# New operation costs and delays in the planner of an attention stage's instruction order

## The chip, the cores and the metric

The kernel runs on one core of a Trainium2 chip. The metric is the device time of one execution in microseconds (us); less is better. A core has engines that each work through their own queue of instructions in order and wait for one another only by semaphores: TensorE (PE, matrix products; PEld is its weight load), VectorE (DVE), ScalarE (ACT) and GpSimd (POOL). SyncE (SP), ACT and POOL issue transfers (DMA). Matrix products write to PSUM, which has eight banks of 512 float32 columns; the other engines read the results from there.

## The reference

One block of a network on 1024 tokens of width 1024: a norm, an input projection, two mixers side by side (a chunkwise mLSTM and a sparse attention), a gated sum of the two through `w_branch`, an output projection, a gated feed-forward layer and a last norm. The edit concerns the attention mixer, which for each block of queries computes

```python
lc = einsum('bgrqd,bgcd->bgrqc', qb, kc_) + bias        # compressed keys, branch 0
o_c = softmax(lc) @ vc_
ls = einsum('bgrqd,bgqnd->bgrqn', qb, k_selected) + bias  # selected blocks, branch 1
o_s = softmax(ls) @ v_selected
lw = einsum('bgrqd,bgkd->bgrqk', qb, k_window) + bias     # window of 512, branch 2
o_w = softmax(lw) @ v_window
out = gate0 * o_c + gate1 * o_s + gate2 * o_w
```

with 8 heads in 2 groups. Sixteen blocks of 64 keys exist and the top 16 are selected, so branch 1 sees all keys up to the query. The mixers' outputs then go through `branch = ys @ w_branch`, are multiplied by `sigmoid(merge)` gates and summed.

## The kernel before

All products are made in split float32 parts: a high part (ACT, line 333 for weights, 1623 for attention) and the remainder, the low part (`wlo` on POOL at line 336, `TL` on DVE at line 1627). A dense product of two split operands is a triplet of matmuls of 512 columns (`mm3`, lines 354 to 356).

**Attention.** The work is cut into 32 units `u` = (pair of heads `p`, block of 128 queries `i`). Each unit has, in order:

- logits, `build_s`: for branches 2 and 0 together ("w") and for branch 1 ("s"), for each head `r` of the pair, matmuls into a PSUM tile `S` (lines 1527 and 1528; two such tiles), then on DVE the bias is added and the row's minimum taken (line 1554, "low"), then on ACT the exponential with its row sum (line 1558);
- a normaliser `rs` for each part (lines 1570 and 1571, DVE) and scalings of the exponentials by it: line 1579 on DVE or, as the list chooses (`alt`), line 1577 on ACT;
- groups of one or two key blocks, `build_t`: transposes on TensorE into a PSUM tile `T` (line 1618; two such tiles), the high part `TH` on ACT, the low part `TL` on DVE, and the products with the values into `obank` (lines 1635 with `TH` and 1638 with `TL`); after a unit's last group ACT copies the result (`os`, line 1644), SP writes one half of it to memory and POOL adds the other half.

**Dense filler.** `c_dense` yields dense triplets one at a time: 12 merge groups of 8 triplets, each evicted by ACT with a bias (line 1456, `mg`), then 16 branch groups of 4 triplets, each evicted by DVE (line 1478, `MX`). All of them accumulate in one PSUM bank, the tile `d` (tag `D`, one buffer), so a group can start only when the one before it has been evicted. The weights of later groups are loaded by SP and split by ACT and POOL on the way (`load`, `split`).

**The order.** The attention's instructions are written in the order that a list planner gives. Every operation (`Op`) has an engine, a duration and what it depends on; the planner keeps one clock for each engine and a delay `LAT` that is added when a result goes to another engine. It repeatedly takes, over the three engines PE, ACT and DVE, the operation that can start first, by priority among those that are ready. On PE, a dense triplet is placed if no attention operation can start within 120 ns of the time at which the triplet could. A scaling goes to ACT only if the planner's DVE clock isn't earlier than ACT's start. When the last logits of a pair of heads are through DVE, `load_pair` issues the next pair's loads, and its first logits are held back for 9000 or 17000 ns of planned time (`pair_at`). When attention's queues are empty, dense triplets are written one after another until at least 13 of the 16 branch groups are done:

```python
while not dn["done"] and (done["n"] < 13 or dn["mid"]):
    ev, evict = next(cd)
```

The branch groups still left (`rest`) are handed to the following stage, which has its own planner and eight banks. The engines don't know of the planned times: they keep the order and the semaphores alone.

Of the kernel before, what the change touches and what calls it, by code (L numbers as in the profile page):

```python
# [15 lines left out]
T = 1024  # L16
# [19 lines left out]
MM = 216.0  # L36
# [136 lines left out]
def body(ctx, tc, a, out):  # L173
# [1249 lines left out]
    with ExitStack() as sc:  # L1423
# [138 lines left out]
        def scale(u, part):  # L1562

            p, i = units[u]
            sl = slice(0, 3, 2) if part == 0 else slice(1, 2)
            gt = GT[:, i, 6 * p:6 * p + 6].rearrange("p (r b) -> p r b", b=3)[:, :, sl]

            def first():
                rs, sm = RS[u][:, :, sl], SUM[u][:, :, sl]
                nc.vector.scalar_tensor_tensor(rs, sm, 1.0e-30, gt, ALU.max, ALU.mult)  # L1570
                nc.vector.reciprocal(rs, rs)

            def one(b, r, eng="DVE"):
                n = (ncmp(i), P * (i + 1), P * nwin(i))[b]
                e = EX[u, "c"][:, r, 0:n] if b == 0 else EX[u, "w" if b == 2 else "s", r][:, 0:n]
                if eng == "ACT":
                    nc.scalar.activation(e, e, AF.Copy, scale=RS[u][:, r, b:b + 1])
                else:
                    nc.vector.tensor_scalar(e, e, RS[u][:, r, b:b + 1], None, ALU.mult)

            todo = [(first, None)]
            for b in ((2, 0) if part == 0 else (1,)):
                for r in range(2):
                    todo.append((lambda eng="DVE", b=b, r=r: one(b, r, eng), (u, b) if r == 1 else None))
            return todo
# [78 lines left out]
                self.eng, self.dur, self.deps, self.emit, self.prio = eng, dur, deps, emit, prio  # L1664
                self.end, self.extra, self.alt = None, extra, alt

        LAT = 180.0
        chain = {"S": [], "T": [], "V": []}
        queues = {"PE": [], "ACT": [], "DVE": []}
        clock = {"PE": 0.0, "ACT": 0.0, "DVE": 0.0}  # L1670

        def push(op):
            queues[op.eng].append(op)
            if op.alt:
                queues[op.alt[0]].append(op)
            return op
# [3 lines left out]
        pv_ops, oc_ops = [], {}  # L1680
# [3 lines left out]
        def build_s(u):  # L1684
            p, i = units[u]
            ops = {}
            for k, r in (("w", 0), ("w", 1), ("s", 0), ("s", 1)):
                b = {"w": 2, "s": 1}[k]
                box = {}

                def emit(u=u, k=k, r=r, box=box):
                    box["low"], box["exp"] = s_job(u, k, r)


                if b == 1:
                    n, parts = P * (i + 1), [min(512, P * (i + 1) - c) for c in range(0, P * (i + 1), 512)]
                else:
                    n, parts = P * nwin(i), [P * (nwin(i) - 1)] * (nwin(i) > 1) + [KB]
                cost = 2 * sum(max(109.0, m / 2.4 + 13.0) for m in parts)
                deps = []  # L1700
                if len(s_free) >= 2:
                    deps.append(s_free[-2])
                if u >= 2:
                    deps.append(("T", u - 2, b))
                if u % 8 == 0 and k == "w" and r == 0:
                    deps.append(("pair", p))
                deps += chain["S"]
                so = push(Op("PE", cost, deps, emit, (u, 1)))
                chain["S"] = [so]
                nr, n = (2, n + ncmp(i)) if b == 2 else (1, n)  # L1710
                tt = push(Op("DVE", nr * 180.0 + 1.044 * n, [so], lambda box=box: box["low"](), (u, 1)))
                s_free.append(tt)
                ex = push(Op("ACT", nr * 290.0 + 0.833 * n, [tt], lambda box=box: box["exp"](), (u, 1)))
                ops[k, r] = ex
                if r == 1:
                    part = 0 if k == "w" else 1
                    de = [ops[k, 0], ex]
                    todo = scale(u, part)
                    rs = push(Op("DVE", 400.0, de, todo[0][0], (u, 2)))
                    bl = [2, 2, 0, 0] if part == 0 else [1, 1]  # L1720
                    scd = {}
                    for bb, (fn, _) in zip(bl, todo[1:]):
                        nn = (ncmp(i), P * (i + 1), P * nwin(i))[bb]
                        scd.setdefault(bb, []).append(push(Op("DVE", 70.0 + 0.522 * nn, [rs], fn, (u, 2),
                                                               alt=("ACT", 230.0 + 0.833 * nn))))
                    for bb, v in scd.items():
                        ops["sc", bb] = v
            return ops

        def build_t(u, ops):  # L1730
            p, i = units[u]
            gr = t_groups(u)
            first = True
            for gi, (part, grp) in enumerate(gr):
                box = {}
                m = len(grp)
                last = gi == len(gr) - 1

                def emit(u=u, gi=gi, grp=grp, last=last, box=box):
                    _, box["hi"], box["lo"], box["pv"] = t_job(u, gi, grp, last)  # L1740

                deps = [o for b, _ in grp for o in ops["sc", b]]
                deps += chain["T"]
                t = push(Op("PE", 214.0 * m, deps, emit, (u, 0), "T"))
                chain["T"] = [t]
                for b, _ in grp:
                    last_t[u, b] = t
                nfr = 256.0 * m
                d2 = [t] + ([pv_ops[-NTH]] if len(pv_ops) >= NTH else [])
                hi = push(Op("ACT", 60.0 + 0.833 * nfr, d2, lambda box=box: box["hi"](), (u, 0)))  # L1750
                lo = push(Op("DVE", 75.0 + 1.044 * nfr, [hi], lambda box=box: box["lo"](), (u, 0)))
                t.extra = ("T", lo)
                dp = [lo]
                if first and u >= 2:
                    dp.append(("OC", u - 2))
                first = False

                def emit_pv(box=box):
                    box["fin"] = box["pv"]()

                dp += chain["V"]
                pv = push(Op("PE", 428.0 * m / 2, dp, emit_pv, (u, 3)))
                chain["V"] = [pv]
                pv_ops.append(pv)
                if last:
                    oc_ops[u] = push(Op("ACT", 270.0, [pv], lambda box=box: box["fin"](), (u, 0)))

        for u in range(NU):
            build_t(u, build_s(u))
# [9 lines left out]
        def ready(op, eng):  # L1779
            t = 0.0  # L1780
            for d in op.deps:
                d = dep_op(d)
                if isinstance(d, tuple):
                    e = pair_at.get(d[1])
                else:
                    e = d.end
                    if e is not None and d.eng != eng:
                        e += LAT
                if e is None:
                    return None  # L1790
                t = max(t, e)
            if op.extra is not None and len(talloc) >= 2:
                e = talloc[-2].end
                if e is None:
                    return None
                t = max(t, e + LAT)
            return t

        dstate = {"gate": 0.0, "op": None}
# [1 line left out]
        dn = {"done": False, "mid": False}  # L1801
        split_end = {}

        def dense_at():
            if dstate["op"] is not None:
                o = dstate["op"]
                return None if o.end is None else max(o.end + LAT, split_end.get(dn["next"][1], 0.0) + LAT)
            return dstate["gate"]

        def place_dense(t):  # L1810
            ev, evict = next(cd)
            dn["mid"] = evict is None
            end = clock["PE"] = t + 3 * MM
            dstate["gate"], dstate["op"] = 0.0, None
            if ev is not None:
                clock["ACT"] = max(clock["ACT"], t) + 950.0
                split_end[ev] = clock["ACT"] + 2600.0
            if evict is not None:
                e = dn["next"][0]
                pe = Op("PE", 3 * MM, [], None, (-1, 0))  # L1820
                pe.end = end
                o = Op(e, 587.0 if e == "ACT" else 680.0, [pe], evict, (-1, 0))
                queues[e].insert(0, o)
                dstate["op"] = o
                dn["next"] = next(cd, None)
                dn["done"] = dn["next"] is None
# [5 lines left out]
        while any(queues.values()):  # L1832
# [19 lines left out]
            cand, e = best  # L1852
# [23 lines left out]
        while not dn["done"] and (done["n"] < 13 or dn["mid"]):  # L1876
            ev, evict = next(cd)
# [830 lines left out]
    bb = {}  # L2708
# [68 lines left out]
```

## Time and profile before

| | |
|---|---|
| median of 3 runs | 1515.35 us (1514.84 to 1516.04) |
| profiled execution, span | 1513.3 us |
| TensorE busy | 1495.8 us (99%) |
| VectorE busy | 1137.3 us (75%) |
| ScalarE busy | 829.1 us (55%) |
| GpSimd busy | 311.3 us (21%) |
| HBM read, written | 185.26 MB, 60.39 MB |

The profile gives the span from the first to the last instruction; the time of the timed runs also holds what lies around the span. Matmuls are pipelined: one of 512 columns is shown with some 390 ns, while the next starts some 227 ns after it, so the busy time of TensorE is no measure of how full it is, but its idle time is idle. Rows of the timeline read: start in us, length in us, engine, line, operation, output <- inputs, sizes, count, and in brackets the engine's idle time before it and what ended it. Rows of the stage windows give, for each engine, the busy time and the number of instructions, then the granted TensorE clock as a share of full speed, the DMA engines' busy share and GB/s. Rows of one line or tile give count, then the shortest, median and longest duration in ns, then the first and the last start in us.

### The profile page before, as it was taken

The numbers are of one execution on the slowest core, as the hardware profiler recorded it, in microseconds if no ns is written. First come the engines' busy times: TensorE is split into PE (matmuls) and PEld (weight loads), VectorE is DVE, ScalarE is ACT, GpSimd is POOL, SyncE is SP. The second block draws the span as 40 slices with busy tenths as digits, with TensorE's granted clock in tenths as the row PEclk, the third lists the DMA queues.
The fourth block names the chain that finished last, engine by engine and source line by source line (L and its number), as shares of the span: only waits on it lengthen the run. The fifth ranks groups of instructions, "written<-read, shape, count | busy, mean of one in ns | idle before, by whom it ended". The sixth has DMA issues, their size and how long they took to land.

```text
span 1513.3 us, 22320 instructions
## 1 busy us (share of the span) xinstructions
PE 1495.8 (99%) x7566; PEld 1262.8 (83%) x7566; DVE 1137.3 (75%) x2411; ACT 829.1 (55%) x1753; POOL 311.3 (21%) x389
## 2 busy tenths in 40 slices
PE   8999999999999999999999999999999999999997
PEld 6888888888889888898888788888888888888886
DVE  8979888867678896989787997555555555785795
ACT  6325666657569796878654674333333333454453
POOL 3000000000312243232101422322222221413310
PEclk9999999999999999999999999999999999999999
DMA  8324664496943378442477966877787776999731
GB/s 278 112 78 143 204 211 147 139 262 188 227 148 73 93 103 235 152 103 50 130 222 181 213 122 134 151 138 138 176 157 138 138 139 139 271 303 177 155 96 56
DMA packets 236133, 239.25 MB, mean 158 GB/s; under 512 B 13458, under 2 KB 179744, under 8 KB 236019
## 3 DMA queue, kind: packets, MB, share of 16 engines
q1 hardware_dynamic: 157296, 169.96, 35.4%
q0 software_dynamic: 78432, 67.48, 29.7%
q8 instruction: 59, 0.97, 0.3%
q14 instruction: 56, 0.45, 0.1%
q10 hardware_dynamic: 290, 0.40, 0.1%
HBM read 185.26 MB, written 60.39 MB: 162 GB/s over the span
## 4 chain that ended last, share of the span: by engine, by line
PE 90%; DVE 4%; issue 2%; DMA 2%; ACT 1%; POOL 0%; SPq 0%; DVEq 0%; POOLq 0%; ACTq 0%
PE PS L355 15%; PE PS L356 15%; PE PS L354 15%; PE bk L354 8%; PE bk L356 8%; PE bk L355 8%; PE T L1618 4%; PE d L354 2%; PE obank L1638 2%; PE obank L1635 2%; PE d L355 2%; PE d L356 2%; DVE UT_float L1966 1%; DMA UT_float<-in_x 1%; DVE quad_float32r L1966 1%
## 5 line engine op out<-in xcount | busy, mean ns | idle before, releaser
L1966 DVE TENSOR_TENSOR UT_float<-PS,UT_float 128x512 f32<-128x512 f32 x115 | 78.2, 689 | 73.7 <-PE PS L356 73.4
L1627 DVE TENSOR_TENSOR TL<-T,TH 128x512 fp32r<-128x512 f32 (+1 forms) x184 | 103.3, 581 | 20.8 <-ACT TH L1623 19.5
L1623 ACT ACTIVATE TH<-T 128x512 fp32r<-128x512 f32 (+1 forms) x184 | 90.6, 510 | 36.2 <-PE T L1618 33.9
L355 PE MATMUL PS<-quad_float32r,whi 128*128 128x512 f32 x272 | 105.9, 390 | 0.6 <-DVE quad_float32r L1966 0.6
L354 PE MATMUL bk<-UT,op 128*128 128x512 f32 x240 | 95.7, 399 | 0.3 <-ACT S L1196 0.3
L356 PE MATMUL bk<-UT,op 128*128 128x512 f32 x240 | 93.6, 390 | 0.0
L355 PE MATMUL bk<-UT,op 128*128 128x512 f32 x240 | 93.5, 390 | 0.0
L355 PE MATMUL PS<-quad_float32r,wlo 128*128 128x512 f32 x208 | 80.9, 389 | 0.0
L355 PE MATMUL PS<-quad_float32r,sl_float32r 128*128 128x512 f32 x200 | 77.8, 389 | 0.0
L354 PE MATMUL PS<-quad_float32r 128*128 128x512 f32 x192 | 75.1, 391 | 0.0
L355 PE MATMUL PS<-quad_float32r 128*128 128x512 f32 x192 | 74.7, 389 | 0.0
L356 PE MATMUL PS<-quad_float32r 128*128 128x512 f32 x192 | 74.7, 389 | 0.0
L354 PE MATMUL bk<-T,op 128*128 128x512 f32 x180 | 72.2, 401 | 0.0
L356 PE MATMUL bk<-T,op 128*128 128x512 f32 x180 | 70.2, 390 | 0.0
L355 PE MATMUL bk<-T,op 128*128 128x512 f32 x180 | 70.2, 390 | 0.0
L1969 ACT ACTIVATE UT_float<-PS 128x512 f32<-128x512 f32 x54 | 31.7, 599 | 69.2 <-PE PS L356 68.6
L355 PEld LDWEIGHTS PS<-quad_float32r,whi 128*128 128x128 f32 x272 | 51.1, 188 | 11.4 <-DVE quad_float32r L1966 1.0
L1650 POOL DMA_DIRECT2D d_yn<-os x32 | 32.5, 1022 | 130.7 <-ACT TH L1623 34.9
L728 ACT ACTIVATE op<-S 128x512 fp32r<-128x512 f32 x52 | 32.4, 628 | 48.3 <-PE bk L355 36.6
L354 PE MATMUL d<-UT,whi 128*128 128x512 f32 x136 | 56.4, 415 | 1.3 <-ACT mg L1456 0.8
L1979 POOL DMA_DIRECT2D sl_float<-in_w_up x28 | 36.5, 1305 | 98.4 <-DVE whi L1966 48.5
L356 PE MATMUL d<-UT,wlo 128*128 128x512 f32 x136 | 53.5, 393 | 0.0
(1464 smaller groups left out, 4874.2 us busy)
## 6 DMA issues: line engine op xcount, KB each, us to landing
rp<-in_w_in SPq DMA_DIRECT2D x27, 512.0 KB, 4.3
d_gu<-UT_float SPq DMA_DIRECT2D x35, 256.0 KB, 3.1
d_rep<-d_row SPq DMA_DIRECT2D x8, 960.0 KB, 6.2
sl_float<-in_w_up POOLq DMA_DIRECT2D x28, 256.0 KB, 4.8
sl_float<-in_w_gate SPq DMA_DIRECT2D x21, 256.0 KB, 3.7
sl_float<-in_w_up SPq DMA_DIRECT2D x21, 256.0 KB, 3.1
rp<-in_w_in SPq DMA_DIRECT2D x20, 256.0 KB, 3.3
d_mg<-S SPq DMA_DIRECT2D x10, 512.0 KB, 7.4
```

The costliest lines, as they stand in the source:

```text
L354: nc.tensor.matmul(ps, ah, bh, start=first, stop=False)
L355: nc.tensor.matmul(ps, ah, bl, start=False, stop=False)
L356: nc.tensor.matmul(ps, al, bh, start=False, stop=last)
L728: step1("ACT", 525.0, lambda: nc.scalar.activation(h, src(), AF.Copy), [r], [b])
L1618: nc.tensor.transpose(pt[:, z, P * r:P * r + P], e, ident)
L1623: nc.scalar.activation(hl[0][:, 0:m], pt[:, 0:m], AF.Copy)
L1627: nc.vector.tensor_tensor(hl[1][:, 0:m], pt[:, 0:m], cast32(hl[0])[:, 0:m], ALU.subtract)
L1635: nc.tensor.matmul(po, vv, th[:, z, :], start=(st[1] + z == 0), stop=False)
L1650: low_half.append(lambda: nc.gpsimd.dma_start(dst, half(1), accum_op=ALU.add))
L1966: return pl.step(alts, lambda e: ENG[e].tensor_tensor(out_(), x(), y(), alu), reads, writes, **kw)
L1969: return pl.step((("ACT", cost),), lambda e: nc.scalar.activation(out_(), x(), fn), reads, writes, **kw)
L1979: pl.step((("Pool", 1000.0),), lambda e: nc.gpsimd.dma_start(dst(), src(), accum_op=ALU.add), reads, writes, lat=lat, kb=kb, nd=1, after=a ...
```

## The change

The costs in the planner are replaced. The operations, their dependencies, the buffers, the gates of the pairs, the rule for dense triplets and the planner itself stay. What can differ in the program is the order of instructions on each engine, which scalings go to ACT and which to DVE, and how many dense triplets are placed where. In the formulas `n` counts columns, `nr` is 2 for "w" and 1 for "s", `m` the blocks of a group, and `MM` is 216.

```diff
-        LAT = 180.0
+        LAT = {"PE": 210.0, "ACT": 150.0, "DVE": 150.0}
...
-                cost = 2 * sum(max(109.0, m / 2.4 + 13.0) for m in parts)
+                cost = 2 * sum(max(109.0, m / 2.4 + 14.0) for m in parts)
...
-                tt = push(Op("DVE", nr * 180.0 + 1.044 * n, [so], lambda box=box: box["low"](), (u, 1)))
+                tt = push(Op("DVE", nr * 85.0 + 1.044 * n, [so], lambda box=box: box["low"](), (u, 1)))
...
-                ex = push(Op("ACT", nr * 290.0 + 0.833 * n, [tt], lambda box=box: box["exp"](), (u, 1)))
+                ex = push(Op("ACT", nr * 275.0 + 0.84 * n, [tt], lambda box=box: box["exp"](), (u, 1)))
...
-                    rs = push(Op("DVE", 400.0, de, todo[0][0], (u, 2)))
+                    rs = push(Op("DVE", 250.0, de, todo[0][0], (u, 2)))
...
-                        scd.setdefault(bb, []).append(push(Op("DVE", 70.0 + 0.522 * nn, [rs], fn, (u, 2),
-                                                               alt=("ACT", 230.0 + 0.833 * nn))))
+                        scd.setdefault(bb, []).append(push(Op("DVE", 130.0 + 0.525 * nn, [rs], fn, (u, 2),
+                                                               alt=("ACT", 185.0 + 0.84 * nn))))
...
-                t = push(Op("PE", 214.0 * m, deps, emit, (u, 0), "T"))
+                t = push(Op("PE", 218.0 * m, deps, emit, (u, 0), "T"))
...
-                hi = push(Op("ACT", 60.0 + 0.833 * nfr, d2, lambda box=box: box["hi"](), (u, 0)))
-                lo = push(Op("DVE", 75.0 + 1.044 * nfr, [hi], lambda box=box: box["lo"](), (u, 0)))
+                hi = push(Op("ACT", 67.0 + 0.834 * nfr, d2, lambda box=box: box["hi"](), (u, 0)))
+                lo = push(Op("DVE", 68.0 + 1.044 * nfr, [hi], lambda box=box: box["lo"](), (u, 0)))
...
-                pv = push(Op("PE", 428.0 * m / 2, dp, emit_pv, (u, 3)))
+                pv = push(Op("PE", 480.0 * m / 2, dp, emit_pv, (u, 3)))
...
-                    oc_ops[u] = push(Op("ACT", 270.0, [pv], lambda box=box: box["fin"](), (u, 0)))
+                    oc_ops[u] = push(Op("ACT", 281.0, [pv], lambda box=box: box["fin"](), (u, 0)))
...
-                        e += LAT
+                        e += LAT[d.eng]
...
-                t = max(t, e + LAT)
+                t = max(t, e + LAT["DVE"])
...
-                return None if o.end is None else max(o.end + LAT, split_end.get(dn["next"][1], 0.0) + LAT)
+                return None if o.end is None else max(o.end, split_end.get(dn["next"][1], 0.0)) + LAT[o.eng]
...
-            end = clock["PE"] = t + 3 * MM
+            end = clock["PE"] = t + 3 * 229.0
...
-                split_end[ev] = clock["ACT"] + 2600.0
+                split_end[ev] = clock["ACT"] + 3000.0
...
-                o = Op(e, 587.0 if e == "ACT" else 680.0, [pe], evict, (-1, 0))
+                o = Op(e, 571.0 if e == "ACT" else 607.0, [pe], evict, (-1, 0))
```

More of the change, by code (lines that the diff above doesn't have):

```diff
@@ L1816, in place_dense @@
                 clock["ACT"] = max(clock["ACT"], t) + 950.0
-                split_end[ev] = clock["ACT"] + 2600.0
+                split_end[ev] = clock["ACT"] + 3000.0
             if evict is not None:
                 e = dn["next"][0]
-                pe = Op("PE", 3 * MM, [], None, (-1, 0))
+                pe = Op("PE", 3 * 229.0, [], None, (-1, 0))
                 pe.end = end
-                o = Op(e, 587.0 if e == "ACT" else 680.0, [pe], evict, (-1, 0))
+                o = Op(e, 571.0 if e == "ACT" else 607.0, [pe], evict, (-1, 0))
                 queues[e].insert(0, o)
```

## The prediction, made before the changed kernel was run

> **What bounds the kernel.** I read the page first, then stage windows, then the waits of the attention stage.
>
> ```profile
> span 1513.3 us, 22320 instructions
> ...
> PE 1495.8 (99%) x7566; PEld 1262.8 (83%) x7566; DVE 1137.3 (75%) x2411; ACT 829.1 (55%) x1753; POOL 311.3 (21%) x389
> ...
> PEclk9999999999999999999999999999999999999999
> ```
>
> TensorE is busy for 99% of the span at the full granted clock. The timed median, 1515.35 us, lies 2.05 us above this span; I take those 2.05 us for what lies around it and sum against the median. The edit touches only the attention list, whose TensorE work (from the first dense product to the last) runs from about 425 to 742.5 us.
>
> ```profile
> core 0: us, PE busy (x) PEld busy (x) DVE busy (x) ACT busy (x) POOL busy (x), PEclk, DMA share, GB/s
> 425.00:742.50 317.50, 314.68 (x2076) 281.49 (x2075) 266.30 (x851) 251.82 (x676) 86.74 (x159) 1.00 0.46 107
> ...
> 501.00:563.00 62.00, 61.42 (x412) 55.20 (x412) 56.78 (x195) 52.87 (x147) 19.78 (x37) 1.00 0.38 61
> 563.00:583.00 20.00, 19.22 (x120) 16.68 (x119) 9.60 (x20) 12.01 (x26) 9.10 (x16) 1.00 1.27 232
> ```
>
> The three numbers that matter are TensorE 314.68, VectorE 266.30 and ScalarE 251.82 us of 317.50. In the stage TensorE is idle for only 317.50 - 314.68 = 2.82 us. Since nothing is added or removed, TensorE's work stays; the edit can only take away stalls or make them. The waits name them:
>
> ```profile
> engine line waited for: us in total, times, longest us
> PE obank L1638 <- DVE TL L1627: 0.9, 2, 0.4
> PE d L354 <- ACT mg L1456: 0.8, 1, 0.8
> PE d L354 <- DVE MX L1478: 0.4, 1, 0.4
> ```
>
> A visible wait understates a stall, because matmuls overlap:
>
> ```profile
> 579.68 0.39 PE L355 MATMUL d<-UT,whi 128*128 128x512 f32 x1
> 579.90 0.39 PE L356 MATMUL d<-UT,wlo 128*128 128x512 f32 x1
> 581.07 0.50 PE L354 MATMUL d<-UT,whi 128*128 128x512 f32 x1 [0.78 <-ACT mg L1456]
> ```
>
> Starts normally lie 0.22 us apart (579.68 to 579.90) and here 1.17, so the 0.78 us wait cost 0.95. Adding that 0.17 us for about a dozen stalls to the 2.82 us, the present stalls are worth some 4.9 us. That is the ceiling of the gain: 0.32% of 1515.
>
> **The change, part by part.** Only the order of instructions can change. Two questions decide: whether the new costs lie nearer the trace relative to TensorE, and how many dense products the list places before attention's own work runs out.
>
> TensorE's costs. Units of work and their real lengths:
>
> ```profile
> L1623 ACT ACTIVATE TH<-T x184: 364/584/604, 432.9 to 738.4; 128x512 fp32r<-128x512 f32 x112, 128x256 fp32r<-128x256 f32 x72
> L354 PE MATMUL d<-UT,whi x136: 387/397/505, 455.5 to 741.7; 128*128 128x512 f32 x136
> L354 PE MATMUL d<-UT,op x16: 388/396/478, 425.4 to 452.7; 128*128 128x512 f32 x16
> ...
> 732.92 0.40 PE L354 MATMUL d<-UT,whi 128*128 128x512 f32 x1
> ...
> 733.61 0.39 PE L354 MATMUL d<-UT,whi 128*128 128x512 f32 x1
> ...
> 718.79 0.40 PE L1635 MATMUL obank<-TH,RND 128*128 128x256 f32 x2
> 719.03 0.40 PE L1638 MATMUL obank<-TL,RND 128*128 128x256 f32 x2
> 719.26 0.40 PE L354 MATMUL d<-UT,whi 128*128 128x512 f32 x1
> ```
>
> There are 184 transposed groups with 2 x 112 + 72 = 296 blocks, and 136 + 16 = 152 dense triplets. A triplet lasts 733.61 - 732.92 = 0.69 us; the list had 3 x 216 = 0.648 and now has 0.687. Value products of a two-block group last 719.26 - 718.79 = 0.47; the list had 0.428 and now 0.480. Sums over the stage: logits 69.4 (the formula over all 32 units) to 69.7, transposes 296 x 0.214 = 63.3 to 296 x 0.218 = 64.5, values 63.3 to 296 x 0.240 = 71.0, dense 152 x 0.648 = 98.5 to 104.4. Planned TensorE time goes from 294.5 to 309.6; traced 314.68. The plan was 6% short and becomes 2% short.
>
> VectorE's and ScalarE's costs.
>
> ```profile
> core 0: us, ACT busy (x), PEclk, DMA share, GB/s
> 425.00:742.50 317.50, 29.57 (x51) 1.00 0.46 107
> ...
> L1554 DVE DVE_READ_ACCUMULATOR2_ANT nx<- x192: 75/83/98, 428.8 to 729.0; 128x1 f32 x192
> ...
> L1570 DVE SCALAR_TENSOR_TENSOR rs<-sm,GT x64: 147/157/687, 430.8 to 731.4; 128x4 f32<-128x4 f32 x32, 128x2 f32<-128x2 f32 x32
> ```
>
> The first row is the scalings (line 1577) that the list gave to ScalarE: 51 of 192, so VectorE has 141. There are 192 bias rows with 4 x 17,456 = 69,824 columns in all (the formula's n over the units), and 64 normaliser pairs. VectorE's plan: bias rows 192 x 180 + 1.044 x 69,824 = 107.5 us, to 89.2 with 85; pairs 64 x 0.400 = 25.6 to 16.0; low parts 92.9 to 91.6 (75,776 columns); the 141 scalings about 34 to 42 (24,000 columns taken off for ScalarE's 29.57 us); 13 dense evictions 8.8 to 7.9. The sum goes from 269 to 247; the trace has 266.30. ScalarE's sum, likewise: exponentials 113.9 to 111.5, high parts 74.2 to 75.5, the rest 56 to 54: 244 to 241 against 251.82. So the old list had VectorE 1% too slow and TensorE 6% too fast; the new one has VectorE 19 us (7%) too fast and TensorE right. The margin that kept VectorE's results waiting for TensorE turns round.
>
> Why the sum misses although single durations are right:
>
> ```profile
> L1579 DVE TENSOR_SCALAR E0w<-E0w,rs x2: 279/282/285, 431.2 to 431.4; 128x128 f32<-128x128 f32 x2
> L1579 DVE TENSOR_SCALAR E8w<-E8w,rs x2: 478/538/597, 504.7 to 505.2; 128x128 f32<-128x128 f32 x2
> L1579 DVE TENSOR_SCALAR E7w<-E7w,rs x2: 565/714/862, 492.3 to 493.1; 128x640 f32<-128x640 f32 x2
> ...
> 505.20 0.98 POOL L1650 DMA_DIRECT2D d_yn<-os  x1
> ```
>
> The same 128-column scaling lasts 282 ns or 538, the latter with GpSimd at work beside it, as at 505.20; E7w's two differ by 0.3 us. A fixed cost near the minimum has no room for that. The Trainium skill, "SBUF — State Buffer", section "SBUF: two separate sides", says that VectorE's two-port operations and GpSimd share a port pair as an exclusive lock, the loser blocking for the whole instruction. The trace agrees in direction (538 against 282); by that rule alone the lateness would be of the size of these rows, a few tenths of a microsecond each time, and would speak for the stalls that I add next.
>
> Term 1, stalls between operations. They are worth 4.9 us now. Bounds: all named waits go (-4.9), or VectorE's shortfall relative to TensorE, 19 - 5 = 14 us, all lands on TensorE (+14). VectorE's new plan is 247 of 310 us, so it still has 20% idle in which to catch up, and only where it runs without a gap does lateness reach TensorE. I take a fifth of 14: +3 us.
>
> Term 2, dense products left over. The list puts a dense triplet in where TensorE would otherwise wait over 120 ns. At the end it forces what is missing up to 13 branch groups: 12 merge groups x 8 + 13 x 4 = 148 triplets. Before, that had just been reached:
>
> ```profile
> 740.05 0.40 PE L1638 MATMUL obank<-TL,RMV 128*128 128x256 f32 x2
> 740.29 0.39 PE L354 MATMUL d<-UT,whi 128*128 128x512 f32 x1
> ...
> 742.34 0.39 PE L354 MATMUL PS<-UT,whi 128*128 128x512 f32 x1
> ```
>
> Three triplets (740.29 to 742.34, 2.05 us) follow the last value product, with no stall. Cheaper VectorE costs make attention's own chain end earlier in the plan, while its TensorE share grows from 196.0 to 205.2 us: less room for dense triplets. If VectorE holds its old share of the plan, 269/294.5 = 91%, attention lasts 247/0.91 = 271 us, the room is 66 us or 96 triplets, and 52 triplets (13 groups of four) are forced. If ScalarE's share holds (244/294.5 = 83%), it lasts 290 us, the room is 85 us or 124 triplets, and 24 (6 groups) are forced. At worst for this theory the room stays and none is. Forced groups have one accumulator bank and nothing between them, so each waits for the eviction of the one before: 0.95 us, the price of the row at 581.07. That gives 0 to 12.4 us; I take 6 groups, ScalarE being the less extreme bound: +5.7 us.
>
> Other parts. Delays of 150 and 210 for 180 shift the transpose loop (TensorE to ScalarE to VectorE to TensorE) by 30 - 30 - 30 = -30 ns; hidden, since TensorE has other work there. The weight split's 3.0 for 2.6 us delays some dense groups, within term 2. GpSimd and SyncE issue the same transfers; their places follow the list's. The pair switch keeps its 9 and 17 us gates:
>
> ```profile
> S<-d_kl POOLq DMA_DIRECT2D x2, 256.0 KB, 12.1
> ...
> 564.99 0.53 POOL L1327 DMA_DIRECT2D S<-d_kl  x1
> ...
> 583.27 0.25 PE L1527 MATMUL S16w<-R,S 128*128 128x192 f32 x1
> ```
>
> The last key load was issued at about 565, lands 12.1 us later, near 577, and is used after 583.27: 6 us of margin, so nothing is charged. One more branch group may go to the next stage, which has eight banks: 0.
>
> Sum: 1515.35 + 3 + 5.7 = 1524.
>
> **The rivals.** (A) Truer costs do what they promise: each operation is queued when its input is there. The four TensorE waits quoted (0.9 + 0.8 + 0.4, with 0.17 us of drain each) go: -2.8 us, 1512.5; with every stall gone 1510.4. For it: the waits on TL and on evictions are just such mistimings. Against it: VectorE's sum moves away from the trace. It decides if TensorE's idle time in the stage falls under 1 us and no forced groups follow. (B) TensorE is packed in either order: stalls change places, the dense count holds: 1515, within 3 us. For it: TensorE's idle time is 2.82 us under costs that were 6% off, so the order seems not to matter much. Against it: VectorE's margin then was on the safe side. (C) The keys of a pair come too late: should the list free the buffers late, each microsecond beyond the 6 us of margin is one of TensorE idle once dense work is out; 4 us over gives 1519. Little speaks for it, as the gate is unchanged.
>
> **How the numbers follow.** My forecast has 0.60, A 0.16, B 0.19, C 0.05. The predicted time is 1524, the likeliest case's. Its own range runs from +2 (few forced groups) to +20 us: 1517 to 1535. Both bounds together would give 1515.35 + 14 + 12.4 = 1542, which I count improbable (under 0.1). Toward A the range reaches 1511.5. What a measurement can tell from no change is 0.2%, 3.03 us. Half of A and a little of B is faster by more, 0.10; the other half, most of B and the low edge of the forecast make 0.31 the same; the rest, 0.59, is slower.
>
> **What would show it.** Right: after the last value product (line 1638) more than three dense triplets stand in a row before line 1966's stage, with a wait on MX (line 1478) of about 0.8 us after each fourth; the attention stage's waits on TL and on scalings grow; fewer scalings than 51 on ScalarE or about as many. Wrong in term 2: three triplets or fewer there. Wrong in term 1: TensorE idle under 2.82 us in the stage. Wrong altogether: a difference that lies outside attention, or TensorE's clock leaving 1.00.

## The result, and the profile after

The changed kernel takes 1532.77 us (median of 4 runs, 1530.69 to 1534.59) against 1515.22 us before (4 runs, 1514.84 to 1516.04): 17.55 us slower, a ratio of 1.0113 with a 95% interval of 1.0101 to 1.0125. The forecast was slower, at 1524 us with a range of 1511.5 to 1535.

The page after, and the attention stage in the same window as before and up to its new end:

```profile
span 1531.1 us, 22319 instructions
...
PE 1505.0 (98%) x7566; PEld 1264.7 (83%) x7566; DVE 1135.9 (74%) x2420; ACT 822.9 (54%) x1744; POOL 309.9 (20%) x389
```

```profile
425.00:742.50 317.50, 307.98 (x2015) 271.07 (x2015) 261.34 (x855) 243.66 (x662) 83.17 (x156) 0.99 0.49 118
425.00:758.10 333.10, 320.35 (x2065) 280.03 (x2065) 264.11 (x859) 247.45 (x669) 86.27 (x160) 0.99 0.50 124
```

The columns are again window, length, busy time and instructions of TensorE, its weight loads, VectorE, ScalarE and GpSimd, the granted clock, DMA share and GB/s. The stage now ends at 758.1 us where it ended at 742.3. TensorE's idle time in it went from 2.82 to 333.10 - 320.35 = 12.75 us, for four triplets fewer (148 against 152; the four moved on to the next stage). The waits name it:

```profile
engine line waited for: us in total, times, longest us
PE d L354 <- DVE MX L1478: 6.8, 9, 0.9
PE obank L1635 <- ACT os L1644: 2.9, 1, 2.9
PE T L1618 <- DVE TL L1627: 2.6, 7, 0.5
```

There are three different losses here. The first is the row of forced groups. In the timeline after the last value product:

```profile
723.88 0.40 PE L1638 MATMUL obank<-TL,RMV 128*128 128x256 f32 x2
724.60 0.50 PE L354 MATMUL d<-UT,whi 128*128 128x512 f32 x1 [0.32 <-DVE MX L1478]
...
727.23 0.39 PE L356 MATMUL d<-UT,wlo 128*128 128x512 f32 x1
728.40 0.50 PE L354 MATMUL d<-UT,whi 128*128 128x512 f32 x1 [0.78 <-DVE MX L1478]
```

Attention's own work ends at 724 us, 16 us earlier than before (740.05), and 36 dense triplets in nine groups follow up to 758.06 us. Behind every fourth triplet TensorE waits for the eviction: eight times 0.95 us from start to start (728.40 - 727.23 less the 0.22 that is normal) and once about 0.5, some 8.2 us. The whole price is higher, because the first matmul after such a wait again takes 0.34 us to the next start where 0.23 is normal: from the last value product to the next stage 34.18 us pass here (723.88 to 758.06), and 24.73 us for the same 36 triplets in e1 below, where nothing waits (726.21 to 750.94). So the tail costs 9.5 us.

The second is one stop at 641 us, with something behind it:

```profile
641.34 0.40 PE L1618 MATMUL T<-cst,E23w 128*128 128x128 f32 x2
644.61 0.51 PE L1635 MATMUL obank<-TH,S 128*128 128x256 f32 x2 [2.88 <-ACT os L1644]
...
644.17 0.38 ACT L1644 ACTIVATE os<-obank 128x256 f32<-128x256 f32 x1 [3.66 <-DMA d_yn<-os]
...
631.58 1.08 POOL L1650 DMA_DIRECT2D d_yn<-os  x1
...
d_yn<-os POOLq DMA_DIRECT2D x1, 64.0 KB, 12.5
UT<-d_y POOLq DMA_DIRECT2D x4, 1024.0 KB, 8.5
```

The value products wait for a free half of `obank`, which waits for ACT to copy a result out (`os`), which waits until the copy of two units before has been written: there are two `os` buffers. That write was issued at 631.58 us and landed 12.5 us later. Just in front of it on GpSimd's queue stand four loads of 1 MB, the mLSTM values for the branch groups (line 1464), and around it the loads of the fourth pair. In the kernel before, the same loads with such a write behind them, but with no pair's loads beside them, were no faster:

```profile
589.20 3.06 POOL L1464 DMA_DIRECT2D UT<-d_y  x4 [6.18 <-PE d L356]
592.25 1.09 POOL L1650 DMA_DIRECT2D d_yn<-os  x1
...
d_yn<-os POOLq DMA_DIRECT2D x1, 64.0 KB, 13.5
...
607.83 0.39 ACT L1644 ACTIVATE os<-obank 128x256 f32<-128x256 f32 x1 [0.56 <-PE obank L1638]
```

That write took 13.5 us and landed near 605.8, but the copy that reuses its buffer came only at 607.83, so nothing waited for it. Slow writes behind the values' load are not new; what is new is that the copy two units later is now due before the write has landed. And then the clock:

```profile
641.00:644.50 3.50, 0.73 (x5) 0.26 (x3) 0.24 (x1) 0.33 (x2) 0.00 (x0) 1.00 0.81 312
645.80:649.20 3.40, 3.40 (x18) 3.31 (x17) 1.39 (x3) 0.98 (x2) 2.55 (x6) 0.50 0.30 39
649.20:655.00 5.80, 5.80 (x44) 5.46 (x43) 4.40 (x26) 4.90 (x19) 0.00 (x0) 1.00 0.19 23
```

After the stop the granted clock is 0.50, the 1.2 GHz level, for 3.4 us: another 1.7 us of work lost. The third loss is the 2.6 us of waits on `TL`, in seven places.

### The profile page after: what moved, and what is told of

The parts are those of the page before. It is cut to its first block, busy times and chain, and to the rows that moved or that the text cites. A ratio compares the mean times of both kernels' runs of the same rounds, so it can differ in the third digit from the quotient of the medians.

```text
span 1531.1 us, 22319 instructions
## 1 busy us (share of the span) xinstructions
PE 1505.0 (98%) x7566; PEld 1264.7 (83%) x7566; DVE 1135.9 (74%) x2420; ACT 822.9 (54%) x1744; POOL 309.9 (20%) x389
## 4 chain that ended last, share of the span: by engine, by line
PE 84%; DVE 8%; DMA 3%; issue 2%; POOL 1%; ACT 1%; SPq 0%; DVEq 0%; POOLq 0%; ACTq 0%
PE PS L355 15%; PE PS L356 15%; PE PS L354 15%; PE bk L354 8%; PE bk L355 8%; PE bk L356 8%; PE T L1618 3%; PE d L354 2%; PE d L356 2%; DVE TL L1627 2%; PE d L355 2%; PE obank L1635 2%; PE obank L1638 2%; DMA UT_float<-in_x 1%; DMA d_yn<-os 1%
## 5 line engine op out<-in xcount | busy, mean ns | idle before, releaser
L1650 POOL DMA_DIRECT2D d_yn<-os x32 | 33.1, 1035 | 155.5 <-DMA d_yn<-os 33.2
L356 PEld LDWEIGHTS bk<-UT,op 128*128 128x128 f32 x240 | 45.0, 188 | 9.5
```

The costliest lines, as they stand in the source:

```text
L356: nc.tensor.matmul(ps, al, bh, start=False, stop=last)
L1650: low_half.append(lambda: nc.gpsimd.dma_start(dst, half(1), accum_op=ALU.add))
```

## The experiments

Each is compared with runs of the kernel before on the same chip (medians of 1515.56 us for e1 to e4, 1515.41 for e5 to e8 and 1515.57 for e9 to e12). My theory was that the tail of forced groups, the stop at 641 us and lateness inside attention add up to the loss. The rival was that VectorE's lateness is all of it.

**e1: two banks for the forced groups.**

```diff
+        TAIL = []          # filled when attention's queues are empty
-            ps = psC.tile([P, 512], ..., tag="D", bufs=1)
+            ps = (that) if not TAIL else psC.tile([P, 2, 2 * P], ..., tag="T", bufs=2).rearrange("p a b -> p (a b)")
```

> The changed kernel, but the dense groups that are forced after attention's queues are empty take turns in the two PSUM banks of tile T, which are free by then, instead of one bank of tile d. Nothing else moves. Theory (the loss is mainly the forced groups' waits for their evictions): the nine waits on MX after the last value product, 8 of about 0.96 us and one of 0.49 from start to start, go, so 8.2 us less than the changed kernel, about 1524.5 us. Rival (VectorE's lateness inside attention is the loss and the tail only shows it): the time stays within 2 us of the changed kernel's 1532.8.

Measured: 1525.82 us, ratio 1.0067 (1.0051 to 1.0084), 7.0 us under the changed kernel. In its waits (the edit moves all later lines by one), those on `MX` are gone and the rest stays:

```profile
PE obank L1636 <- ACT os L1645: 5.1, 1, 5.1
PE T L1619 <- DVE TL L1628: 2.6, 7, 0.4
```

The theory's share was 8.2 us, and the tail is 9.5 us shorter in the trace; but in this profile the stop had grown from 2.9 to 5.1 us, which takes 2.2 back and leaves 7.3, near the 7.0 measured. Why the stop grew is not known. The rival (within 2 us) falls.

**e2: the values' load one merge group later.**

```diff
-            yield from merge(14, 1, {0: values})
-            yield from merge(15, 1, {0: lambda: split(n + 2)})
+            yield from merge(14, 1, {})
+            yield from merge(15, 1, {0: lambda: (values(), split(n + 2))[1]})
```

> The changed kernel, but the 4 MB load of the mLSTM values (line 1464) is issued one merge group later, at the first product of the last merge group. Theory (that load, made late by the missing dense groups, now meets the loads of the fourth pair, slows the write of an attention result, and through os and obank stops TensorE for 3.1 us at 641 us, after which the granted clock is at its lower level for 3.4 us): the stop and the lower clock go, 3.1 + about 1.5 us less, about 1528 us. Rival (the pair's own loads are enough to slow that write): the wait of ACT's os on the write of d_yn stays, 1532.8 us.

Measured: 1528.25 us, ratio 1.0083 (1.0068 to 1.0098), 4.5 us under the changed kernel, as the theory had it. The wait on `os` is gone, the waits on `MX` (6.8 us, 9 times) and `TL` (2.6, 7 times) are the same, and the clock stays at its upper level until 1523.5 us, in the kernel's last microseconds, where it falls in the kernel before too. So the values' load, which the missing dense groups had moved from 589 us to 624 to 631 us, made that stop. The rival falls: the fourth pair's loads alone don't make it.

**e3: both edits.**

> Both edits on the changed kernel: two banks for the forced groups and the values' load one merge group later. Theory: the gains add, 8.2 + 4.6 = 12.8 us less, about 1520 us; the 5 us that stay above the kernel before are then the stalls between operations inside attention. Rival (the stalls inside attention are small): 1515 us.

Measured: 1518.75 us, ratio 1.0020 (1.0011 to 1.0030; 10 runs): 14.0 us of the 17.5 are back, which is the 9.5 of the tail and the 4.5 of e2 (e3 lies 9.50 us under e2). What TensorE still waits for, and its stage:

```profile
engine line waited for: us in total, times, longest us
PE T L1619 <- DVE TL L1628: 2.6, 7, 0.4
PE obank L1639 <- DVE TL L1628: 0.2, 1, 0.2
PE S26s L1528 <- DVE nx L1555: 0.2, 1, 0.2
...
425.00:743.80 318.80, 315.67 (x2064) 278.96 (x2063) 264.13 (x859) 246.39 (x667) 85.65 (x159) 1.00 0.50 124
```

All three are waits for VectorE, and 3.2 us above the kernel before remain. That is the size of the forecast's first term, but these waits don't make up the 3.2 us. They sum to 3.0 us; the kernel before has 2.5 us of named waits (the 0.9, 0.8 and 0.4 that the prediction shows, and two of 0.2). TensorE is idle for 318.80 - 315.67 = 3.13 us in this stage, against 2.82 before. Waits on `TL` have taken the place of waits for dense evictions. Where the rest of the 3.2 us goes stays open.

**e4 to e6: parts of the change alone.** e4 is the kernel before with the delays alone (first line of the diff), e5 with TensorE's durations alone, e6 with VectorE's alone.

> The kernel before with the delays alone changed (210 ns from TensorE, 150 from ScalarE and VectorE, for 180); all durations as before. Theory (delays do not matter, durations do): all 13 branch groups are reached as before, no forced waits, 1515.2 us within 3. Rival (shorter delays after VectorE leave operations without margin): 3 us or more above the kernel before.

> The kernel before with TensorE's new durations alone (transposes, values, logits, dense triplets); ScalarE's, VectorE's durations and the delays as before. The list then leaves five branch groups to be forced. Theory (fewer dense triplets fit, so forced groups wait; VectorE keeps its margin in absolute terms): four or five waits of 0.96 us on MX at the end, stalls inside attention about as before, 1519 to 1521 us. Rival (truer TensorE costs help by themselves): 1515 us or less.

> The kernel before with VectorE's new durations alone. The list then leaves four branch groups to be forced. Theory: TensorE and VectorE are now both about 6% too fast in the plan, so neither is late against the other inside attention; what is lost are the forced groups' waits, about 3.8 us: 1519 us. Rival (VectorE's minimal durations alone make it late inside attention): waits on TL and on scalings of 4 us more than before on top, 1523 us or more.

Measured: e4 1521.45 us, ratio 1.0036 (1.0023 to 1.0049); e5 1531.23, 1.0104 (1.0089 to 1.0119); e6 1539.18, 1.0154 (1.0139 to 1.0169). All three expectations missed, all to the slow side. The times of e4 and e6 lie where their rivals put them, but e6's rival also named waits on `TL` and on scalings of 4 us more, and the waits on `TL` are 2.8 us in all. The parts alone cost 5.9, 15.8 and 23.8 us, and all changes together 17.5, so they don't add; ScalarE's durations alone were not run. The largest wait of e5 and of e6:

```profile
PE d L354 <- ACT mg L1456: 7.5, 3, 7.2
...
PE obank L1635 <- ACT os L1644: 14.3, 1, 14.3
PE d L354 <- DVE MX L1478: 3.2, 4, 0.9
```

The expected waits on `MX` are there (e6: 3.2 us, 4 times), but a single stop outweighs them. Its place is the switch to the third pair. ACT's copy `os` there, in the order before, e4, e5, e6, e7 (below):

```profile
579.36 0.39 ACT L1644 ACTIVATE os<-obank 128x256 f32<-128x256 f32 x1 [1.63 <-issue]
...
580.74 0.38 ACT L1644 ACTIVATE os<-obank 128x256 f32<-128x256 f32 x1 [4.31 <-DMA d_yn<-os]
...
581.59 0.38 ACT L1644 ACTIVATE os<-obank 128x256 f32<-128x256 f32 x1 [11.02 <-DMA d_yn<-os]
...
580.84 0.38 ACT L1644 ACTIVATE os<-obank 128x256 f32<-128x256 f32 x1 [15.71 <-issue]
...
579.77 0.38 ACT L1645 ACTIVATE os<-obank 128x256 f32<-128x256 f32 x1 [7.76 <-issue]
```

In five different orders the copy starts between 579.4 and 581.6 us; what differs is how long ACT had stood before it, 1.6 to 15.7 us. (In the changed kernel and in e8 it comes a little earlier, at 573.93 and 577.91, after 2.41 and 1.57 us.) The adding write that it needs stands on GpSimd's in-order queue behind the twelve loads of the third pair (in e6 the loads are issued from 557.87 us, the write at 572.23). ACT, standing, does nothing else, and TensorE waits: in e5 for the dense eviction `mg` behind the copy, in e6 for the copy itself, with the value products. In the kernel before, the copy's wait of 1.63 us costs TensorE nothing that shows. The dense stall behind 579.90 us, which the prediction shows, isn't the copy's doing, though the two lie close together: `mg` starts when the triplet has ended, after ACT has been free for 0.58 us.

```profile
580.33 0.69 ACT L1456 ACTIVATE mg<-d,COLS 128x512 f32<-128x512 f32 x1 [0.58 <-PE d L356]
```

That stall is the plain price of the single bank, as in the tail. The planner knows of neither the write nor the time it takes to land.

**e7 and e8: the changed kernel with margin.** Both have e3's edits. e7 also counts VectorE's and ScalarE's durations 8% longer and lets a dense triplet in wherever TensorE would wait at all; e8 takes the old durations of VectorE and ScalarE.

```diff
-                    if cand is None or cand[2] > dst + 120.0:
+                    if cand is None or cand[2] > dst + 0.0:
-            op.end = clock[e] = st + op.dur
+            op.end = clock[e] = st + op.dur * (1.0 if e == "PE" else 1.08)
```

> The changed kernel with the two edits of e3, and VectorE's and ScalarE's durations counted 8% longer in the plan (the trace's sums of 266 against 247 us), and a dense triplet placed wherever TensorE would wait at all rather than over 120 ns. The list then reaches all 13 branch groups by itself. Theory (margin on VectorE and room for the dense triplets are what the change lost): no forced waits, TensorE idle in the stage under 2.8 us, 1512 to 1516 us. Rival (the order is as good or bad by chance): anything up to 1520 us.

> The changed kernel with the two edits of e3 and the old durations of VectorE and ScalarE (the old, longer ones), so TensorE's durations and the delays are the new ones. Four branch groups are forced, in two banks. Theory: the waits on TL that e3 kept (2.6 us) go, 1514 to 1517 us. Rival (the delays alone cost 6 us, as in e4, whatever the durations): 1520 us.

Measured: e7 1523.16 us, ratio 1.0050 (1.0033 to 1.0066); e8 1520.15, 1.0034 (1.0021 to 1.0047). Both missed. e7's loss is the row at 579.77 above: one wait of 6.9 us behind it and a lower clock until 586.9 us. e8's largest wait, 2.5 us on `TL` before 669.17 us, is the same stop in another place: ACT's `TH`, from which `TL` is made, stands behind a copy that waits for its write, and 3.4 us at the lower clock follow.

```profile
666.61 0.38 ACT L1645 ACTIVATE os<-obank 128x256 f32<-128x256 f32 x1 [3.34 <-DMA d_yn<-os]
```

The other waits on `TL` in e8 sum to 1.2 us, 4 times, against 2.6 us, 7 times, in e3: fewer, as its theory had it, but the times don't tell what margin is worth.

**e9 to e12: the adding write at once.** If the write stands behind the loads, issue it with the unit's own copy: e9 on the changed kernel, e10 on e6, e11 on e7, e12 on the kernel before.

```diff
-                        low_half.append(lambda: nc.gpsimd.dma_start(dst, half(1), accum_op=ALU.add))
+                        nc.gpsimd.dma_start(dst, half(1), accum_op=ALU.add)
```

> The changed kernel, but the adding write of a unit's second half (GpSimd, line 1650) is issued with the unit's own copy os, where it was issued at the next unit's. It then no longer stands behind the next pair's loads on GpSimd's queue. Theory (the stop at 641 us is os waiting for the adding write of two units before, which stood behind the values' load): the 2.9 us wait on os and the lower clock after it go, about 1528 us as in e2; the nine waits of the tail stay. Rival (the transfers themselves are slow at the switch, wherever the write stands in the queue): the wait stays, 1532 us.

> e6 (VectorE's durations alone) with the adding write at once. Theory: the 14.3 us stop on os at 567 us and the lower clock until 587.4 us (about 3 us of work lost after the stop) go, 17 us less, about 1522 us; what is left above the kernel before are four forced waits (3.8 us) and single waits. Rival (as in e9): a stop of 7 us or more stays, 1530 us or more.

> e7 (new costs, 8% margin, two banks, values later) with the adding write at once. Theory: the 7.3 us stop at 574 us and the lower clock until 586.9 us (2.7 us lost) go, 10 us less, about 1513 us. Rival (margin is worth nothing): 1518 us or more, with waits on VectorE's results spread over the stage.

> The kernel before with the adding write at once. Theory: its one wait of os on that write (1.63 us before 579.36 us) and the dense stall behind it (0.95 us) go, about 1514.5 us. Rival (GpSimd, now waiting for each first half to land, delays the weights' splits and the memsets behind it): 1516 us or more.

Measured: e9 1545.11 us, ratio 1.0195 (1.0179 to 1.0210); e10 1543.40, 1.0180 (1.0163 to 1.0197); e11 1529.91, 1.0092 (1.0077 to 1.0107); e12 1529.07, 1.0090 (1.0074 to 1.0105). The edit is bad everywhere; on the kernel before it costs 13.5 us. All four theories missed; e9's time lies above both ranges, those of e10 to e12 where their rivals put them. The reason given for the stop holds in part, the remedy falls. In e10 ACT's copy still stands 9.9 us for its write, and TensorE 8.1 us behind it. In e12 the wait of `os` on the write is gone, but the dense stall of 0.78 us is still there, so the write had not caused it. In e9 TensorE's wait on `os` at 641 us is gone, and in its place it has the first two of these rows; the last two are e12's:

```profile
PE T L1618 <- POOL E24c L1546: 2.5, 1, 2.5
PE S16w L1528 <- DMA R<-d_kl: 2.5, 1, 2.5
...
PE S8w L1527 <- DMA S<-d_ql: 2.7, 2, 2.2
PE T L1618 <- DVE E19w L1579: 1.8, 1, 1.8
```

GpSimd now stands until each unit's first half has been made and has landed (in e9 seven waits of its `d_yn` on the first half's landing sum to 58.3 us, against 33.2 in the changed kernel), and it is late with the next pair's keys and queries and with the memsets (line 1546). Neither place on its queue that was tried suits the write. A third `os` buffer, or the values' loads on another queue, was not tried. No version tried beats the kernel before.

## Why the prediction was right or wrong

**Right: direction, and what decides.** The changed kernel is slower, and 14.0 of the 17.5 us are two sorts of stops that e1 to e3 take away, with 1.7 us at the lower clock behind one of them. The ceiling on the gain (4.9 us) was not touched. One of the signs for "wrong altogether" did occur: TensorE's clock left 1.00, for 3.4 us. It belongs to the stop that the sum had left out.

**Term 2, the forced groups: right mechanism, size 9.5 us where 5.7 was taken.** The price for each was about right, 0.95 us in the wait and some 0.1 us more behind it; there were nine groups, between the bounds of 6 (ScalarE's share) and 13 (VectorE's) of which I took the lower. The last value product at 723.88 us comes 299 us after the stage's start. The bounds said 271 and 290 us for the plan, and a longer attention should have left fewer forced groups than six, not more; the 299 us hold the stop and stalls, which no plan has, so they confirm neither bound, and why it was nine is not shown. What was said to show the mechanism did: a wait on `MX` behind each fourth triplet. The reading of the kernel before was off by one group: with 152 triplets it places 14 branch groups, so the three triplets after its last value product finish the fourteenth. The list gave 42 scalings to ScalarE, fewer than 51:

```profile
core 0: us, ACT busy (x), PEclk, DMA share, GB/s
425.00:742.50 317.50, 25.30 (x42) 0.99 0.49 118
```

**Term 1, stalls inside attention: 3.2 us remain in e3 where 3 was taken, but the agreement is in part luck.** The waits that e3 keeps are all for VectorE, as argued, and those on `TL` grew as forecast, from 0.9 to 2.8 us (2.6 and 0.2); no wait on scalings appeared. But the waits on evictions inside attention went, so all named waits grew by 0.5 us only, and TensorE's idle time in e3's stage by 0.3. The other 2 us and more have no cause shown, and whether GpSimd's work beside VectorE has a part in the late `TL` no run tells. That the short durations cause the waits on `TL` isn't shown either: e8, with the old ones, has fewer of them, but its order met another stop and its time did not get below e3's.

**Wrong: the step "GpSimd and SyncE issue the same transfers; their places follow the list's", charged at nothing.** It cost the stop at 641 us and the lower clock, 4.5 us by e2. The places did follow the list's, and that was the harm: a load tied to a dense group came 35 to 40 us later, and the write behind it, as slow as before (12.5 and 13.5 us), was now needed before it had landed. I had looked for the danger at the pair switch in the keys (rival C, 6 us of margin), which were in time; it was the write of the results, which the same queue carries, and the two `os` buffers that wait for it.

**Wrong: delays "hidden, since TensorE has other work there".** Alone they cost 5.9 us (e4): waits for VectorE's `nx` of 1.9 us, a dense stall of 1.4 us at the third pair's switch, and a lower clock after it. The loop sum of -30 ns said nothing of what another order meets elsewhere. What share the delays have in the changed kernel's own loss no run shows.

The sum by what was measured: 9.5 + 4.5 + 3.2 = 17.2 us of 17.5; the rest lies within what the runs of the kernel before differ by (medians of 1515.22 and 1515.56). Rival A is excluded by the runs; B too, as the number of dense triplets placed fell by a quarter. Open: what the best order under true costs would be once the write's queue is modelled, and what makes up e3's last 3.2 us.

## What to carry to other kernels

Truer costs in a list planner don't make a truer plan when the plan leaves out a resource: here one DMA queue, two buffers, and the filler's tail, which is written after the plan has ended. Before changing costs, ask which things are paced by how many filler pieces get placed (loads hooked to them, what is forced at the end), and count them by hand from the planner's sums; that gave the sign here. And read the filler's tail first: nine single-bank evictions were 9.5 of the 17.5 us lost, and two banks that were free took that back.

## What the runs showed of the hardware that was not expected

After the one stop of 2.9 us the granted clock was 0.50 for 3.4 us, while through the tail with its waits of 0.8 us it was 1.00, as in its last part here:

```profile
742.50:758.00 15.50, 12.27 (x51) 8.90 (x50) 2.77 (x4) 3.69 (x7) 3.00 (x5) 1.00 0.72 258
```

In e6 the granted clock fell during the 14.3 us stop, near 570 us, and was 0.50 up to 587.4 us, 6 us beyond the stop's end. The Trainium skill, "TensorE: Matmul & The Clock Gate", Part 1, says that the gate passes half the pulses after TensorE has been idle; the 0.50 behind these stops agrees. A 64 KB adding write took 12.5 us to land behind the four loads of 1 MB (13.5 in the kernel before), and 2.9 us at the median of the changed kernel's 32 such writes:

```profile
DMA to landing us min/median/max: 2.7/2.9/12.5
```
